# Attention scores of 64-row operands as paired products, in a one-core encoder layer

## The chip, the core and the metric

The kernel runs on one core of a Trainium2 chip. The metric is the time of one execution on the device, in microseconds (us); the profile is of one further execution, taken by the hardware profiler. TensorE appears in the profile as PE (products) and PEld (loads of the stationary operand), VectorE as DVE, ScalarE as ACT, GpSimd as POOL, SyncE as SP.

## What is computed

One encoder layer over 256 tokens of width 2048, in float32: adaLN modulation, a mixer with two attention groups of eight heads each, an output projection, a squared-ReLU feed-forward of width 8192, and a final norm. The change is in the scores of both groups:

```python
def diff_attention(q, k, v, lam):
    scale = DIFF_HEAD_DIM ** -0.5
    def block(qb):
        s = jnp.einsum('bqhcd,bkhcd->bhcqk', qb * scale, k).astype(jnp.float32)
        p = jax.nn.softmax(s, axis=-1)
        a = p[:, :, 0] - lam32 * p[:, :, 1]
        return jnp.einsum('bhqk,bkhe->bqhe', a.astype(v.dtype), v)

def mla_attention(q_nope, q_rope, k_nope, k_rope, v):
    scale = (MLA_NOPE_DIM + MLA_ROPE_DIM) ** -0.5
    def block(args):
        qn, qr = args
        s = (jnp.einsum('bqhd,bkhd->bhqk', qn, k_nope)
             + jnp.einsum('bqhr,bkr->bhqk', qr, k_rope)).astype(jnp.float32) * scale
        p = jax.nn.softmax(s, axis=-1)
        return jnp.einsum('bhqk,bkhe->bqhe', p.astype(v.dtype), v)
```

A differential head has two maps (c = 0, 1), each from queries and keys of 64 elements. A latent head adds a product over 128 elements (the plain part) and one over 64 rotary elements whose key is shared by all heads.

## The kernel before

All tensors lie with 128 partitions. Tokens come in two blocks of 128 (`t` = 0, 1). Weights stream from memory in pieces of 1 MB through a ring of buffers (`raw_tile`); for the large projections each piece is split on ScalarE and VectorE into a high and a low part (`split`, L124 and L125) and multiplied in three products (`block`, L299). The adaLN vectors are made beside that, from a stream of their own: part of it as products on TensorE with 32 columns in each of four column groups of the array (`ada_cols`, L319, and `ada_pe`, L382), part of it as multiply-adds on VectorE (`ada_acc`, L366) that GpSimd or TensorE then sums over partitions.

The stages follow each other: adaLN and input projection, latent attention's preparation (`latent_prep`), the attention itself, the output projection (`mixer_out`), the feed-forward. `run(...)` mixes generators by weights and so sets the order in which the instructions are written; a scheduler with tile dependencies then orders each engine's queue, and each engine works through its queue in that order.

`attention()` goes through heads 0 to 7 of both groups together. For each even head it first makes keys, values and queries of a latent pair (`latent_kv`, `latent_q`), then, for each head, the latent scores, the differential scores and, two heads later (`LAG` = 2), the transposes of the probabilities and the products with the values.

The scores are float32 products without the split, and each is two passes in the trace. The pieces that the change touches:

- Differential scores, L650 to L675. `diff_heads_T` transposes query and key of a head into one bank `pt` (`dT`), both maps above each other: rows 0 to 63 are map 0, rows 64 to 127 map 1. The query goes to `qT` (`dqT`, L657). The key goes into `kz` in two halves, each beside zeros that GpSimd wrote once: map 0 by ScalarE (L659), map 1 by VectorE (L660). `diff_scores` then makes one product of 128 rows and 512 columns per token block, with both maps beside each other in one bank `ds` (L667).
- Latent scores, L600 to L613. Per head and token block one product of 128 rows for the plain part (L605) and one of 128 rows for the rotary part (L606), into the same bank `ms`. The rotary query `qr` holds both heads of a pair above each other, and the key `krz` holds the shared key once for each head beside zeros.
- `softmax_rows`, L591 to L598: the negated row maximum on VectorE (L593), its product with the scale (L594), two exponentials on ScalarE with that as bias and the scale as factor (L596), a reciprocal of the sums (L598). For the differential maps follow the factor `nlam` (L671), a scaling on ScalarE (L672) and a multiply-add on VectorE (L673).

## Time and profile before

| | |
|---|---|
| median of 3 runs | 1188.09 us (1187.98 to 1190.48) |
| span of the profiled execution, first to last instruction | 1182.8 us |
| its own time | shown by the span alone; the runs' median is 5.3 us above it |
| instructions | 14208 |
| TensorE busy, products | 1140.9 us, 96% |
| TensorE busy, weight loads | 916.1 us, 77% |
| VectorE busy | 811.8 us, 69% |
| ScalarE busy | 552.0 us, 47% |
| GpSimd busy | 53.3 us, 5% |
| read from memory | 294.47 MB, 251 GB/s over the span |

Shares over the span mix stages with different limits, so the busy time is also read by stretches. A product that has been issued overlaps the one before it: the distance between two starts, not the duration of one, says how long TensorE is taken by it.

### The profile page before, as it was taken

What the parts mean: (1) busy time and instruction counts of PE and PEld (TensorE: products, weight loads), DVE (VectorE), ACT (ScalarE), POOL (GpSimd) and SP (SyncE); (2) the same over time, 40 slices, a digit from 0 to 9 for tenths busy, and PEclk for the clock granted to TensorE, in tenths of its full rate; (3) what the DMA queues carried; (4) which work ended last, traced back from release to release, by engine and by line L of the source; (5) the groups of instructions that cost most, each with busy time, mean ns of one, the idle gap of its engine ahead of it and who ended that gap; (6) DMA issues with size and microseconds to landing.
All of it is one profiled execution on the core that took longest, in us unless ns stands there. A gap on an engine that the chain in (4) does not pass through costs nothing.

```text
span 1182.8 us, 14208 instructions
## 1 busy us (share of the span) xinstructions
PE 1140.9 (96%) x5502; PEld 916.1 (77%) x5502; DVE 811.8 (69%) x1013; ACT 552.0 (47%) x812; POOL 53.3 (5%) x50
## 2 busy tenths in 40 slices
PE   5999999998999998999999999999999999999996
PEld 4666778865778887888888888888888888888875
DVE  3245559996899878875755666676686676555776
ACT  3432334547774445445544444344344344344343
POOL 1000000112101000000000000000020002000000
PEclk9999999999999998999999999999999999999998
DMA  9999973786888786996565646667767867556531
GB/s 348 392 390 369 356 305 130 254 313 223 292 313 299 281 315 236 330 343 219 185 220 178 209 155 205 236 232 266 276 222 275 281 237 251 184 181 203 182 104 72
DMA packets 94196, 297.50 MB, mean 252 GB/s; under 512 B 5712, under 2 KB 16167, under 8 KB 93488
## 3 DMA queue, kind: packets, MB, share of 16 engines
q1 hardware_dynamic: 94016, 296.56, 71.1%
q8 instruction: 43, 0.70, 0.2%
q14 instruction: 25, 0.20, 0.0%
q10 hardware_dynamic: 112, 0.03, 0.0%
HBM read 294.47 MB, written 2.10 MB: 251 GB/s over the span
## 4 chain that ended last, share of the span: by engine, by line
PE 60%; DVE 1%; issue 1%; ACT 0%; ACTq 0%; POOLq 0%; POOL 0%; DVEq 0%
PE f_p L299 51%; PE f1a_p L299 7%; PE fT L903 1%; PE h2T L856 0%; DVE x_res L921 0%; DVE acc L920 0%; DVE acc L918 0%; PE shift_f_pc L407 0%; PE scale_f_pc L407 0%; DVE acc L924 0%; ACT sq L927 0%; DVE h2t L829 0%; ACT acc L840 0%; ACT acc L948 0%; PE h2Ts L845 0%
## 5 line engine op out<-in xcount | busy, mean ns | idle before, releaser
L125 DVE TENSOR_TENSOR f_w_lo<-f_r,f_w_hi 128x1024 fp32r<-128x1024 f32 x224 | 278.1, 1250 | 197.4 <-ACT f_w_hi L124 197.0
L124 ACT CAST f_w_hi<-f_r 128x1024 fp32r<-128x1024 f32 x224 | 236.2, 1054 | 317.8 <-PE f_p L299 300.9
L299 PE MATMUL f_p<-f_w_hi,h 128*128 128x512 f32 x768 | 209.4, 391 | 0.0
L299 PEld LDWEIGHTS f_p<-f_w_hi,h 128*128 128x128 f32 x768 | 143.4, 188 | 29.3 <-ACT h L859 0.2
L299 PE MATMUL f_p<-f_w_hi,fh 128*128 128x512 f32 x512 | 158.6, 390 | 0.3 <-ACT fh L905 0.3
L299 PE MATMUL f_p<-f_w_lo,fh 128*128 128x512 f32 x512 | 158.8, 389 | 0.0
L299 PE MATMUL f_p<-f_w_hi,fl 128*128 128x512 f32 x512 | 158.8, 389 | 0.0
L299 PE MATMUL in_p<-in_w_hi,hT 128*128 128x512 f32 (+1 forms) x512 | 141.5, 389 | 2.8 <-ACT hT L354 2.7
L299 PE MATMUL f_p<-f_w_lo,h 128*128 128x512 f32 x384 | 119.0, 390 | 0.0
L299 PEld LDWEIGHTS in_p<-in_w_hi,hT 128*128 128x128 f32 x512 | 95.9, 191 | 26.9 <-ACT in_w_hi L124 4.3
L299 PEld LDWEIGHTS f_p<-f_w_hi,fh 128*128 128x128 f32 x512 | 96.0, 188 | 21.9 <-DVE acc L918 1.4
L299 PEld LDWEIGHTS f_p<-f_w_hi,fl 128*128 128x128 f32 x512 | 96.0, 188 | 20.0
L299 PEld LDWEIGHTS f_p<-f_w_lo,fh 128*128 128x128 f32 x512 | 96.1, 188 | 19.8
L125 DVE TENSOR_TENSOR in_w_lo<-in_r,in_w_hi 128x1024 fp32r<-128x1024 f32 (+1 forms) x64 | 73.2, 1169 | 44.5 <-ACT in_w_hi L124 44.2
L299 PEld LDWEIGHTS f_p<-f_w_lo,h 128*128 128x128 f32 x384 | 72.0, 188 | 14.8
L299 PE MATMUL in_p<-in_w_lo,hT 128*128 128x512 f32 (+1 forms) x256 | 79.5, 389 | 1.7 <-DVE in_w_lo L125 1.5
L124 ACT CAST in_w_hi<-in_r 128x1024 fp32r<-128x1024 f32 (+1 forms) x64 | 62.8, 1011 | 34.9 <-PE in_p L299 27.3
L299 PE MATMUL f1a_p<-f1a_w_hi,h 128*128 128x512 f32 x256 | 70.1, 394 | 0.0
L299 PEld LDWEIGHTS in_p<-in_w_lo,hT 128*128 128x128 f32 x256 | 48.1, 191 | 12.4 <-DVE in_w_lo L125 5.2
L299 PEld LDWEIGHTS f1a_p<-f1a_w_hi,h 128*128 128x128 f32 x256 | 48.4, 190 | 9.9
L124 ACT CAST f1a_w_hi<-f1a_r 128x1024 fp32r<-128x1024 f32 x32 | 33.6, 1054 | 42.3 <-PE f1a_p L299 34.9
L124 ACT CAST out_w_hi<-out_r 128x1024 fp32r<-128x1024 f32 x32 | 33.6, 1053 | 38.4 <-PE out_p L299 38.4
(323 smaller groups left out, 1380.0 us busy)
## 6 DMA issues: line engine op xcount, KB each, us to landing
f_r<-w_ff SPq DMA_DIRECT2D x112, 1024.0 KB, 5.5
in_r<-w_in SPq DMA_DIRECT2D x24, 1024.0 KB, 11.4
sc__r<-w_ada SPq DMA_DIRECT2D x16, 1024.0 KB, 10.4
sh__r<-w_ada SPq DMA_DIRECT2D x16, 1024.0 KB, 6.7
gate_m_r<-w_ada SPq DMA_DIRECT2D x16, 1024.0 KB, 5.9
scale_f_r<-w_ada SPq DMA_DIRECT2D x16, 1024.0 KB, 5.1
out_r<-w_out SPq DMA_DIRECT2D x16, 1024.0 KB, 8.2
shift_f_r<-w_ada SPq DMA_DIRECT2D x16, 1024.0 KB, 6.3
```

The costliest lines, as they stand in the source:

```text
L124: s.copy(hi, src)
L125: v.tensor_tensor(lo, src, hi.bitcast(F32), ALU.subtract)
L299: pe.matmul(ps[t][j][:, 0:nw], lhsT=lhs[(lk0 + kk) // 8][:, (lk0 + kk) % 8, t * P:(t + 1) * P], rhs=rhs[:, n0:n0 + nw], start=(kk == 0 and ...
L903: pe.transpose(pt[:, i * S + t * P:i * S + (t + 1) * P], rl[:, t, (kp + i) * P:(kp + i + 1) * P], ident)
```

## The change

- The zero-padded keys `kz` and `krz` go, with their clears on GpSimd.
- `diff_heads_T` puts query and key into one tile `qkT`, both by ScalarE, and multiplies the query by the scale on the way. `diff_scores` takes rows 0 to 63 for map 0 and rows 64 to 127 for map 1: four products of 64 rows and 256 columns per head, map by map into two banks, so that a bank holds one map for both token blocks where it held both maps of one block. The two maps are combined after both softmaxes.
- `latent_scores` does both heads of a pair at once, with a bank each: per token block the rotary products of 64 rows, one per head, then the two plain products of 128 rows. The rotary key `kr` is one copy of the key above another.
- The scales go into the operands: the differential one into the query, the latent one into the plain key (the copy in `latent_kv`) and into `kr` (`latent_prep`). `softmax_rows` loses its scaling of the maxima.

```diff
@@ -60,6 +60,7 @@
 FW = (42.0, 2.0, 2, 2)
 PRI_ATT = 0
 
+MLA_SCALE = float((NOPE + ROPE) ** -0.5)
 TWO_PI = 2.0 * np.pi
 INV_2PI = float(np.float32(1.0 / TWO_PI))
 RND = 12582912.0
@@ -483,7 +484,7 @@
     mla_g = act.tile([P, D], F32, tag="x1", name="mla_g")
     swap = mla_g[:, 0:P]
     qx = mla_g[:, 256:512]
-    krz = mla_g[:, 512:1024].rearrange("p (a q) -> p a q", a=2)
+    kr = mla_g[:, 512:768]
     qn_ring = [mla_g[:, 1024 + i * 512:1024 + (i + 1) * 512].rearrange("p (a q) -> p a q", a=2) for i in range(2)]
     for i in range(4):
         g.tensor_copy(swap[:, i * 32:(i + 1) * 32], ident[:, (i ^ 1) * 32:(i ^ 1) * 32 + 32])
@@ -496,7 +497,6 @@
         return t1, t2
 
     def latent_prep():
-        g.memset(krz, 0.0)
         kpd = []
         for t in range(T):
             for nm, o, n in (("q", 0, QL), ("kv", QL, KVL)):
@@ -530,8 +530,8 @@
                 pe.transpose(pt[:, o * S + t * P:o * S + (t + 1) * P],
                              kpd[t][:, 2 * o:2 * o + 2, :].rearrange("p a b -> p (a b)"), ident)
         t1, t2 = rope_T(pt, "kr")
-        v.tensor_tensor(krz[0:64, 0, :], t1[0:64, :], t2[0:64, :], ALU.add)
-        v.tensor_tensor(krz[64:128, 1, :], t1[64:128, :], t2[64:128, :], ALU.add)
+        v.tensor_tensor(t1, t1, t2, ALU.add)
+        s.mul(kr, t1, MLA_SCALE)
         yield 0.5
 
     def three(ps, pairs):
@@ -551,7 +551,7 @@
             three(pk[:, i * S:(i + 1) * S],
                   [((hi[:, k, i, 0:P], lo[:, k, i, 0:P]), (cq_hi[:, nq + k, :], cq_lo[:, nq + k, :]))
                    for k in range(nkv)])
-        s.copy(kn[hp % 2], pk.rearrange("p (h q) -> p h q", h=2))
+        s.mul(kn[hp % 2], pk.rearrange("p (h q) -> p h q", h=2), MLA_SCALE)
         yield 1.3
         pv = bank(f"pv{hp}")
         for t in range(T):
@@ -588,29 +588,35 @@
         v.tensor_tensor(qr, t1, t2, ALU.add)
         hold.append((qn, qr))
 
-    def softmax_rows(sc, scale, p, sums, name):
+    def softmax_rows(sc, p, sums, name):
         nm = small.tile([P, 2], F32, tag="nm", name=name + "_nm")
         v.tensor_reduce(nm, sc, AX.X, ALU.max, negate=True)
-        v.tensor_scalar(nm, nm, scale, None, op0=ALU.mult)
         for i in range(2):
-            s.activation(p[:, i, :], sc[:, i, :], AF.Exp, bias=nm[:, i:i + 1], scale=scale,
+            s.activation(p[:, i, :], sc[:, i, :], AF.Exp, bias=nm[:, i:i + 1], scale=1.0,
                          accum_out=sums[:, i:i + 1])
         v.reciprocal(sums, sums)
 
-    def latent_scores(h, qn, qr):
-        i = h % 2
-        kh = kn[h // 2 % 2][:, i, :]
-        sc = bank(f"ms{h}", "mm")
-        for t in range(T):
-            pe.matmul(sc[:, t * S:(t + 1) * S], lhsT=qn[:, i, t * P:(t + 1) * P], rhs=kh, start=True, stop=False)
-            pe.matmul(sc[:, t * S:(t + 1) * S], lhsT=qr[:, t * P:(t + 1) * P], rhs=krz[:, i, :],
-                      start=False, stop=True)
-        p = p_buf()
-        sums = small.tile([P, 2], F32, tag="sums", name=f"msum{h}")
-        softmax_rows(sc.rearrange("p (t k) -> p t k", t=2), float((NOPE + ROPE) ** -0.5), p, sums, f"m{h}")
-        for t in range(T):
-            s.mul(p[:, t, :], p[:, t, :], sums[:, t:t + 1])
-        return p
+    def latent_scores(hp, qn, qr):
+        scs = [bank(f"ms{2 * hp + i}", "mm") for i in range(2)]
+        for t in range(T):
+            for i in range(2):
+                hs = slice(64 * i, 64 * i + 64)
+                pe.matmul(scs[i][:, t * S:(t + 1) * S], lhsT=qr[hs, t * P:(t + 1) * P], rhs=kr[hs, :],
+                          start=True, stop=False)
+            for i in range(2):
+                pe.matmul(scs[i][:, t * S:(t + 1) * S], lhsT=qn[:, i, t * P:(t + 1) * P], rhs=kn[hp % 2][:, i, :],
+                          start=False, stop=True)
+        ps = []
+        for i in range(2):
+            h = 2 * hp + i
+            p = p_buf()
+            sums = small.tile([P, 2], F32, tag="sums", name=f"msum{h}")
+            softmax_rows(scs[i].rearrange("p (t k) -> p t k", t=2), p, sums, f"m{h}")
+            for t in range(T):
+                s.mul(p[:, t, :], p[:, t, :], sums[:, t:t + 1])
+            ps.append(p)
+            yield 1.8
+        lps.extend(ps)
 
     def latent_probs_T(h, p):
         tp = bank(f"mtp{h}")
@@ -653,33 +659,38 @@
             for t in range(T):
                 pe.transpose(pt[:, o * S + t * P:o * S + (t + 1) * P],
                              qk[t][:, o * 1024 + h * P:o * 1024 + (h + 1) * P], ident)
-        qT = at.tile([P, S], F32, tag="dqT", name=f"dqT{h}", bufs=2)
-        s.copy(qT, pt[:, 0:S])
-        z = kz[h % 2]
-        s.copy(z[0:64, 0, :], pt[0:64, S:2 * S])
-        v.tensor_copy(z[64:128, 1, :], pt[64:128, S:2 * S])
-        return qT, z
-
-    def diff_scores(h, qT, z):
-        ps = []
-        for t in range(T):
-            sc = bank(f"ds{h}{t}", "mm")
-            pe.matmul(sc, lhsT=qT[:, t * P:(t + 1) * P], rhs=z.rearrange("p a b -> p (a b)"), start=True, stop=True)
+        qkT = qkT_ring[h % 2]
+        s.mul(qkT[:, 0, :], pt[:, 0:S], float(DH ** -0.5))
+        s.copy(qkT[:, 1, :], pt[:, S:2 * S])
+        return qkT
+
+    def diff_scores(h, qkT):
+        scs = [bank(f"ds{h}{c_}", "mm") for c_ in range(2)]
+        for t in range(T):
+            for c_ in range(2):
+                hs = slice(64 * c_, 64 * c_ + 64)
+                pe.matmul(scs[c_][:, t * S:(t + 1) * S], lhsT=qkT[hs, 0, t * P:(t + 1) * P], rhs=qkT[hs, 1, :],
+                          start=True, stop=True)
+        ps, sm = [], []
+        for c_ in range(2):
             p = p_buf()
-            sums = small.tile([P, 2], F32, tag="sums", name=f"dsum{h}{t}")
-            softmax_rows(sc.rearrange("p (t k) -> p t k", t=2), float(DH ** -0.5), p, sums, f"d{h}{t}")
-            v.tensor_tensor(sums[:, 1:2], sums[:, 1:2], nlam, ALU.mult)
-            s.mul(p[:, 0, :], p[:, 0, :], sums[:, 0:1])
-            v.scalar_tensor_tensor(p[:, 0, :], p[:, 1, :], sums[:, 1:2], p[:, 0, :], op0=ALU.mult, op1=ALU.add)
+            sums = small.tile([P, 2], F32, tag="sums", name=f"dsum{h}{c_}")
+            softmax_rows(scs[c_].rearrange("p (t k) -> p t k", t=2), p, sums, f"d{h}{c_}")
             ps.append(p)
-        return ps
-
-    def diff_probs_T(h, ps):
+            sm.append(sums)
+        v.tensor_scalar(sm[1], sm[1], nlam, None, op0=ALU.mult)
+        for t in range(T):
+            s.mul(ps[0][:, t, :], ps[0][:, t, :], sm[0][:, t:t + 1])
+            v.scalar_tensor_tensor(ps[0][:, t, :], ps[1][:, t, :], sm[1][:, t:t + 1], ps[0][:, t, :],
+                                   op0=ALU.mult, op1=ALU.add)
+        return ps[0]
+
+    def diff_probs_T(h, p):
         tp = bank(f"dtp{h}")
         pT = pT_buf()
         for t in range(T):
             for kt in range(T):
-                pe.transpose(tp[:, kt * S + t * P:kt * S + (t + 1) * P], ps[t][:, 0, kt * P:(kt + 1) * P], ident)
+                pe.transpose(tp[:, kt * S + t * P:kt * S + (t + 1) * P], p[:, t, kt * P:(kt + 1) * P], ident)
         s.copy(pT, tp.rearrange("p (k q) -> p k q", k=2))
         return pT
 
@@ -769,7 +780,7 @@
     if LAG > 1:
         p_ring += [lat[t][:, 0:512].rearrange("p (a q) -> p a q", a=2) for t in range(T)]
         p_ring.append(at.tile([P, 2, S], F32, tag="px", name="px"))
-    kz = [asc[1][:, 1024 + i * 512:1024 + (i + 1) * 512].rearrange("p (a q) -> p a q", a=2) for i in range(2)]
+    qkT_ring = [asc[1][:, 1024 + i * 512:1024 + (i + 1) * 512].rearrange("p (a q) -> p a q", a=2) for i in range(2)]
     cnt = {"p": 0, "pT": 0}
 
     def p_buf():
@@ -780,8 +791,8 @@
         cnt["pT"] += 1
         return at.tile([P, 2, S], F32, tag="pT", name=f"pT{cnt['pT']}", bufs=2)
 
-    for z in kz:
-        g.memset(z, 0.0)
+    lps = []
+
     def attention():
         live = []
         for i in range(H + LAG):
@@ -789,13 +800,13 @@
                 if i % 2 == 0 and i > 0:
                     yield from latent_kv(i // 2)
                     yield from latent_q(i // 2, hold)
-                lp = latent_scores(i, *hold[i // 2])
-                yield 1.8
+                if i % 2 == 0:
+                    yield from latent_scores(i // 2, *hold[i // 2])
             if i >= LAG:
                 lT = latent_probs_T(i - LAG, live[0][0])
                 yield 0.5
             if i < H:
-                live.append((lp, diff_scores(i, *diff_heads_T(i))))
+                live.append((lps[i], diff_scores(i, diff_heads_T(i))))
                 yield 2.0
             if i >= LAG:
                 dT = diff_probs_T(i - LAG, live.pop(0)[1])
```

Two places of the instruction order bear on the prediction. The first is TensorE at heads 2 and 3, before (`ms2` and `ms3` are the latent score banks of these heads, `ds20` and `ds21` the differential ones of head 2, first by token block, then by map; `mo` and `do` are products with the values):

```order
L606 MATMUL ms2_2258<-mla_g_1502,qr1_2252 128x256
L605 MATMUL ms2_2258<-mla_f_1501,mla_g_1502 128x256
L606 MATMUL ms2_2258<-mla_g_1502,qr1_2252 128x256
L667 MATMUL ds20_2294<-asc1_2052,dqT2_2290 128x512
L667 MATMUL ds21_2306<-asc1_2052,dqT2_2290 128x512
L627 MATMUL mo0_2325<-pT1_2283,mla_f_1501 128x256 x2
L690 MATMUL do0_2330<-dv0_93,pT2_2319 128x128
L690 MATMUL do0_2330<-dv1_94,pT2_2319 128x128
L690 MATMUL do0_2330<-dv0_93,pT2_2319 128x128
L690 MATMUL do0_2330<-dv1_94,pT2_2319 128x128
L605 MATMUL ms3_2337<-mla_f_1501,mla_g_1502 128x256
```

and now, from the second token block's latent scores on:

```order
L604 MATMUL ms2_2247<-mla_g_1502,qr1_2241 128x256
L604 MATMUL ms3_2248<-mla_g_1502,qr1_2241 128x256
L607 MATMUL ms2_2247<-mla_f_1501,mla_g_1502 128x256
L607 MATMUL ms3_2248<-mla_f_1501,mla_g_1502 128x256
L672 MATMUL ds20_2293<-asc1_2051 128x256
L672 MATMUL ds21_2294<-asc1_2051 128x256
L672 MATMUL ds20_2293<-asc1_2051 128x256
L672 MATMUL ds21_2294<-asc1_2051 128x256
L633 MATMUL mo0_2323<-pT1_2284,mla_f_1501 128x256 x2
L701 MATMUL do0_2328<-dv0_93,pT2_2317 128x128
```

The latent scores of head 3 stood behind head 2's differential scores and the value products; now they alternate with head 2's, two rotary products of 64 rows and two plain ones of 128, and the differential scores of head 2 follow as four products that alternate between two banks.

The second is VectorE while the first two heads are scored, before (`kv_lo` and `q_0_lo` are low parts of the next latent pair's weights, `m_nm` and `d_nm` the row maxima):

```order
L125 TENSOR_TENSOR kv_lo<-kv_r_2163,kv_hi 128x1024
L594 TENSOR_SCALAR d_nm<-d_nm 128x2
L598 RECIPROCAL dsum_2085<-dsum_2085 128x2
L593 TENSOR_REDUCE m_nm<-ms_2107 128x2
L671 TENSOR_TENSOR dsum_2085<-dsum_2085,nlam 128x1
L593 TENSOR_REDUCE d_nm<-ds_2130 128x2
L673 SCALAR_TENSOR_TENSOR asc_2051<-asc_2051,dsum_2085 128x256
L594 TENSOR_SCALAR m_nm<-m_nm 128x2
L594 TENSOR_SCALAR d_nm<-d_nm 128x2
L593 TENSOR_REDUCE d_nm<-ds_2142 128x2
L598 RECIPROCAL dsum_2097<-dsum_2097 128x2
L125 TENSOR_TENSOR q_0_lo<-q_r_2197,q_0_hi 128x768
```

and now:

```order
L593 TENSOR_REDUCE m_nm<-ms_2053 128x2
L367 SCALAR_TENSOR_TENSOR gate_m_1671<-gate_m_r_2071,cs,gate_m_1671 128x1024
L593 TENSOR_REDUCE m_nm<-ms_2054 128x2
L367 SCALAR_TENSOR_TENSOR gate_m_1671<-gate_m_r_2071,cs,gate_m_1671 128x1024
L597 RECIPROCAL msum_2063<-msum_2063 128x2
L126 TENSOR_TENSOR kv_lo<-kv_r_2152,kv_hi 128x1024
L597 RECIPROCAL msum_2075<-msum_2075 128x2
L126 TENSOR_TENSOR q_0_lo<-q_r_2186,q_0_hi 128x768
L126 TENSOR_TENSOR q_1_lo<-q_r_2186,q_1_hi 128x768
L593 TENSOR_REDUCE d_nm<-ds_2090 128x2
```

The scalings of the maxima between the rows are gone, and both low parts of the query weight stand ahead of the first maximum of the differential scores.

## Rows read from the trace of the kernel before

**Rows 1.** The page, part 1 (engine, busy us, share, instructions) and part 4 (chain).

```profile
PE 1140.9 (96%) x5502; PEld 916.1 (77%) x5502; DVE 811.8 (69%) x1013; ACT 552.0 (47%) x812; POOL 53.3 (5%) x50
...
PE 60%; DVE 1%; issue 1%; ACT 0%; ACTq 0%; POOLq 0%; POOL 0%; DVEq 0%
PE f_p L299 51%; PE f1a_p L299 7%; PE fT L903 1%; PE h2T L856 0%; DVE x_res L921 0%; DVE acc L920 0%; DVE acc L918 0%; PE shift_f_pc L407 0%; PE scale_f_pc L407 0%; DVE acc L924 0%; ACT sq L927 0%; DVE h2t L829 0%; ACT acc L840 0%; ACT acc L948 0%; PE h2Ts L845 0%
```

**Rows 2.** Stretches of the span: length; busy us by engine; granted clock, DMA share, GB/s.

```profile
50.00:100.00 50.00, 48.29 (x269) 31.85 (x267) 21.01 (x29) 17.41 (x25) 0.00 (x0) 1.00 1.05 386
250.00:300.00 50.00, 44.85 (x257) 30.33 (x256) 39.02 (x88) 37.62 (x107) 11.72 (x6) 1.00 0.68 235
300.00:350.00 50.00, 48.12 (x287) 36.01 (x286) 47.13 (x91) 37.95 (x114) 3.59 (x1) 1.00 0.91 327
350.00:400.00 50.00, 49.46 (x241) 41.18 (x240) 43.86 (x52) 24.08 (x30) 5.70 (x3) 1.00 0.84 304
600.00:700.00 100.00, 100.00 (x450) 82.59 (x449) 54.53 (x54) 45.36 (x52) 0.00 (x0) 1.00 0.58 190
```

**Rows 3.** TensorE's waits at 250 to 350 us: total us, times, longest.

```profile
PE pq L542 <- DVE q_lo L125: 3.4, 1, 3.4
PE dtp L682 <- ACT qk L693: 1.5, 1, 1.5
```

**Rows 4.** Timeline of TensorE, 252 to 260 us: start, duration, instruction, count.

```profile
252.10 0.59 PE L605 MATMUL ms<-mla_f,mla_g 128*128 128x256 f32 x2
252.53 0.59 PE L606 MATMUL ms<-mla_g,qr 128*128 128x256 f32 x2
253.06 1.07 PE L382 MATMUL gate_m_pg<-gate_m_r,cpad 128*32 128x512 f32 x8
...
257.83 1.98 PE L667 MATMUL ds<-asc,dqT 128*128 128x512 f32 x4
```

**Rows 5.** Timeline of TensorE, 330 to 350 us.

```profile
332.63 1.88 PE L667 MATMUL ds<-asc,dqT 128*128 128x512 f32 x4
334.35 1.05 PE L690 MATMUL do<-dv,pT 128*128 128x128 f32 x8
```

**Rows 6.** Score products, by form, 250 to 350 us: busy us, mean ns.

```profile
L667 PE MATMUL ds<-asc,dqT 128*128 128x512 f32 x32 | 15.5, 606 | 0.1
...
L606 PE MATMUL ms<-mla_g,qr 128*128 128x256 f32 x32 | 9.8, 389 | 0.0
```

**Rows 7.** Timeline of TensorE, 88 to 94 us (input projection, adaLN, input projection).

```profile
88.31 1.07 PE L299 MATMUL in_p<-in_w_hi,hT 128*128 128x512 f32 x4
...
89.67 0.61 PE L299 MATMUL in_p<-in_w_hi,hT 128*128 128x512 f32 x2
90.22 1.92 PE L319 MATMUL sh__pg<-sh__r,cpad 128*32 128x512 f32 x16
92.07 1.21 PE L299 MATMUL in_p<-in_w_hi,hT 128*128 128x512 f32 x4
```

**Rows 8.** VectorE's groups by form, 245 to 350 us: busy us, mean ns, idle.

```profile
L594 DVE TENSOR_SCALAR d_nm<-d_nm 128x2 f32<-128x2 f32 x16 | 5.0, 319 | 0.0
...
L660 DVE COPY asc<-dT 64x256 f32<-64x256 f32 x8 | 3.4, 428 | 0.6 <-ACT asc L659 0.3
...
L671 DVE TENSOR_TENSOR dsum<-dsum,nlam 128x1 f32<-128x1 f32 x16 | 2.4, 151 | 0.1
```

**Rows 9.** ScalarE's group of query copies, same view and stretch.

```profile
L657 ACT COPY dqT<-dT 128x256 f32<-128x256 f32 x8 | 3.1, 392 | 0.4 <-PE dT L654 0.4
```

**Rows 10.** Timeline of VectorE, 261 to 270 us.

```profile
262.18 2.21 DVE L594 TENSOR_SCALAR d_nm<-d_nm 128x2 f32<-128x2 f32 x1
...
268.64 0.93 DVE L125 TENSOR_TENSOR q_lo<-q_r,q_hi 128x768 fp32r<-128x768 f32 x1
...
269.87 0.15 DVE L594 TENSOR_SCALAR d_nm<-d_nm 128x2 f32<-128x2 f32 x1
```

**Rows 11.** Timeline of GpSimd, 250 to 300 us.

```profile
262.06 6.55 POOL L393 PARTITION_ALL_REDUCE gate_m<-gate_m  x2 [9.62 <-DVE d_nm L593]
```

## Prediction

> **What bounds the kernel now.** I read the page first. TensorE is busy for 96% of the span and VectorE for 69%; the chain that ended last runs through 60% of the span and is TensorE throughout [rows 1]. So time that TensorE gains in a stage where it is the engine that runs on can reach the end, if nothing after it was waiting for something else. The busy time by stretches says where that holds [rows 2]: the attention stage lies at about 250 to 350 us, with TensorE busy 44.85 and 48.12 of each 50 us, VectorE 39.02 and 47.13; behind it TensorE goes on at 49.46 of 50, and in the feed-forward (600 to 700 us) at 100 of 100, all at a granted clock of 1.00 (2.4 GHz). The DMA queues moved 386 GB/s at 50 to 100 us and 327 and 304 GB/s at 300 to 400 us, so the weights can come a few microseconds sooner. The waits of TensorE inside the stage name what else can end last [rows 3]: 3.4 us once for a half of a query weight on VectorE, 1.5 us once before a transpose of probabilities. A saving in TensorE's work is therefore worth nearly its face value; a wait that the change creates costs the same.
>
> **TensorE: the paired products.** A float32 product stands in the trace as two passes. The passes of 256 columns follow each other 0.215 us apart (two start at 252.10, the next two at 252.53 [rows 4]), those of 512 columns 0.43 us (four from 332.63 to 334.35 [rows 5]). There are 32 passes of 512 columns of the differential scores (`ds`, L667) and 32 of 256 columns of the rotary half of the latent scores (`ms`, L606) [rows 6]: 13.8 + 6.9 = 20.6 us. The change makes each a product over 64 rows, 256 columns, in the upper or lower half of the array, and gives the two of a pair a bank each. If both halves stream at once, the 20.6 us become 10.3. No row shows two row halves at once. The nearest row is the adaLN product that uses four groups of 32 columns: eight passes of 512 columns take 1.07 us there, against 1.98 us for four of `ds` [rows 4], so four groups did stream side by side, both passes included. I take full overlap: 10.3 us gained. The other end is no overlap: nothing.
>
> **TensorE: the changes of tiling.** The same adaLN product shows what it costs to go from the whole array to a part and back. Dense passes follow each other 0.23 us apart (four take 1.07, two 0.61); the last dense one began at 89.67 + 0.23 = 89.90, the first tiled one at 90.22 [rows 7]: 0.32, so 0.1 too late. On the way back four dense passes take 1.21 us instead of 1.07 [rows 7], because the first weights are loaded in the open, and they begin about 0.1 us after the 16 tiled passes (4 x 0.43 us) are through. A first weight load of 128 columns in the open shows again in `ds` after the adaLN product, where four passes take 1.98 instead of 1.88 us [rows 4, 5]. So a change of tiling costs about 0.1 of idling and 0.1 of open weight load, 0.2 us each way. The Trainium skill, TensorEngine Tiling (Array Packing), section Tiling Modes, says that changing the mode, not merely the tile, drains TensorE; the trace agrees, with the 0.1 us above. By that rule the sum is the one below; without it the gain would be the whole 10.3 us.
>
> In the new order there are 15 stretches of 64-row products: two for each of the four latent pairs (rotary, plain, rotary, plain) and seven for the eight differential heads, the first two heads standing together. That is 30 changes, one of which takes the place of one that was there: 29 x 0.2 = 5.8 us. Bounds for one change: 0 (products of unlike lines in the same tiling follow without a gap [rows 5]) and 0.4 (twice the measured). It is instructive that the latent half pays nothing: per token block it saves 0.43 us and buys two changes for 0.4. The gain is the differential half. TensorE's work: -10.3 + 5.8 = -4.5 us.
>
> **VectorE and ScalarE.** Gone from VectorE are 24 scalings of the row maxima (16 of them of `ds`), 0.15 us each where nothing disturbs them [rows 10], 8 copies of half a key, 0.43 us each, and 8 of 16 small products of 0.15 us [rows 8]: 3.6 + 3.4 + 1.2 = 8.2 us of an engine that is busy 86 of 100 us here. A scaling stood between each row maximum and its exponentials, and a key copy on VectorE ahead of each `ds`; both sat in VectorE's queue among adaLN's long passes. ScalarE now copies the whole key (128 rows by 256) where it copied half of it, at the 0.39 us that the query copy takes [rows 9], and scales `kr` once: some 0.5 us in all, on an engine with 12 of 50 us free [rows 2]. The removed GpSimd clears waited for nothing that anyone needed. These edits cost nothing while that cover lasts. On the debit side, a head's two maps must now both be through their softmax before either token block is combined, and both heads of a latent pair are scored before the first transposes; what would then be late is a transpose of probabilities two heads on, 1.5 us in one place now.
>
> Of TensorE's waits, 3.4 us are one event: GpSimd's two all-reduces run from 262.06 for 6.55 us [rows 11], a VectorE operation on 2 columns takes 2.21 us meanwhile, and the query half that TensorE needs is begun only at 268.64 [rows 10]. In the new VectorE order both query halves stand ahead of the first `ds` maxima, so they may be done before the all-reduces start, or be caught by them. Of 3.4 + 1.5 = 4.9 us I take 1.5 as gone: between all of it and nothing, nearer to nothing, because the new order opens waits of its own at this place (the key and query copies of the first two differential heads now stand behind the first latent pair's softmax on ScalarE).
>
> **The sum.** -4.5 - 1.5 = -6.0 us. The profiled execution has a span of 1182.8 us, 5.3 below the runs' median of 1188.09; what lies around the span is taken as unchanged. Span 1176.8, time **1182.1 us**.
>
> **Rivals.**
> - *The waits go too.* All 4.9 us vanish, since VectorE loses a tenth of its work: -4.5 - 4.9, 1178.7. For it: the 3.4 us are one collision. Against: the all-reduces still run, with new neighbours.
> - *Half overlap.* If passes start strictly in program order, the second pass of the first product holds up the second product: a pair takes 3 rounds of 0.215 us instead of 2, four products 5 instead of 4. Saved: 8 x 0.65 + 8 x 0.215 = 6.9 instead of 10.3; less 5.8 and with the 1.5: 1185.5. Against it speak the eight passes in 1.07 us [rows 4], which strict order with 0.43 us per round would not allow. The Trainium skill, TensorE: Matmul & The Clock Gate, Part 3, states that matmuls are strict FIFO in start and end; how a float32 product's two passes are queued it does not say.
> - *The gain becomes a wait.* TensorE arrives sooner, but the softmax chain of VectorE and ScalarE ends when it did: about 1188. Against: those engines lose work too.
> - *Slower: the pairs do not pack.* The products over 64 rows run one after the other, so the change does not do what it says. Place: the `ms` rotary pairs and all `ds`. TensorE keeps its 20.6 us and pays 5.8 us: 1193.9. It decides from the point where less than 5.8 of the 10.3 us is saved. Against: the column groups overlap, and each half has its own bank; for: no row shows it for rows.
>
> **How the numbers follow.** Forecast 0.53, waits too 0.14, half overlap 0.11, gain becomes a wait 0.10, slower 0.12. Faster by over 0.2% (2.4 us, about what a measurement of this kernel tells from no change) means below 1185.7: nearly all of the forecast, the first rival, and half of the second: 0.70. Within: 0.17. Slower: 0.13. Range: down to the free changes of tiling (-10.3 - 1.5: 1176.3) and up past the costly ones (0.4 each: -10.3 + 11.6 - 1.5, 1187.9) and the lost gain to 1189.5; the unpacked case is left out.
>
> **What would show it.** Right: the two products of a pair start within some 0.02 us; the four `ds` of a head take about 1.1 us with their change in, instead of 1.72; the rotary pair 0.43; plain products after it start 0.1 us late with an open load; no scaling between maximum and exponential; from 400 us on the same work, shifted by 6 us. Wrong: `ds` passes 0.215 us apart one by one, or new waits of TensorE over 3 us before `ds`, `pk` or `dtp`.

## The result, and the profile after

The changed kernel takes **1193.39 us** (median; 1192.95 to 1194.88), the kernel before, run beside it, 1188.03: a ratio of 1.0055, 95% interval 1.004 to 1.0071. It is slower by half a per cent, where 1182.1 was forecast. The profiled execution has a span of 1191.1 us against 1182.8.

Those two spans are 8.3 us apart, the medians 5.4. The table ahead of the prediction takes 5.3 us as lying between span and time; in every run whose span stands beside its time the difference is 1.7 to 1.9 us. So the profiled execution of the kernel before was a quick one of its kind: beside the experiments the same kernel ran 80 times, with a median span of 1186.0 us and a mean granted clock of 0.989 over the span (0.986 to 0.992), where the profiled execution has 1182.8 and 0.991. The four runs of the changed kernel all have 0.982.

TensorE's line on the page, and the granted clock in the span's 40 slices (page, parts 1 and 2, of the changed kernel):

```profile
PE 1144.5 (96%) x5534; PEld 918.7 (77%) x5534; DVE 807.3 (68%) x972; ACT 552.5 (46%) x813; POOL 50.2 (4%) x47
...
PEclk9999999988989998999999999999999999999999
```

TensorE is busy 3.6 us *longer* than in [rows 1], with less to do. The clock's tenths show four slices at 8, three of them in the attention stage (in the kernel before one at the mixer's end, and the last slice of all). The same stretches as [rows 2] (length; busy us of PE, PEld, DVE, ACT, POOL; granted clock; DMA share; GB/s), and then every stretch at a granted clock of 0.50 in which TensorE works:

```profile
250.00:300.00 50.00, 44.55 (x255) 30.68 (x254) 33.55 (x67) 37.47 (x106) 10.68 (x4) 0.86 0.61 212
300.00:350.00 50.00, 42.69 (x273) 29.90 (x272) 43.13 (x62) 32.79 (x95) 3.45 (x1) 0.96 0.84 309
...
25.09:31.92 6.83, 5.81 (x17) 5.54 (x18) 2.82 (x4) 1.96 (x4) 0.00 (x0) 0.50 1.03 393
260.58:267.41 6.83, 5.41 (x22) 4.02 (x23) 6.61 (x7) 3.41 (x8) 5.49 (x3) 0.50 0.94 333
287.89:294.71 6.82, 6.06 (x22) 4.41 (x23) 1.86 (x5) 3.27 (x10) 3.23 (x1) 0.50 0.41 156
345.91:352.74 6.83, 6.35 (x23) 4.70 (x24) 5.27 (x8) 5.12 (x14) 0.00 (x0) 0.50 0.80 279
451.73:458.56 6.83, 4.32 (x15) 3.01 (x16) 5.14 (x11) 5.42 (x15) 1.31 (x2) 0.50 0.47 154
550.72:554.13 3.41, 3.41 (x10) 2.62 (x11) 2.84 (x7) 1.83 (x5) 0.00 (x0) 0.50 0.52 154
```

The kernel before has two of them, at the start and behind the mixer:

```profile
25.60:32.43 6.83, 6.03 (x17) 5.77 (x18) 2.59 (x4) 2.18 (x4) 0.00 (x0) 0.50 1.03 392
445.50:452.33 6.83, 5.10 (x16) 3.69 (x17) 5.15 (x10) 5.33 (x12) 0.81 (x1) 0.50 0.46 156
```

If half of the busy time at 1.2 GHz counts as lost against 2.4 GHz, a span splits into three parts that can be compared: the loss (half the busy time of such stretches), the work (busy time of the page less the loss), the idle time (span less busy time). Before: loss (6.03 + 5.10) / 2 = 5.6, work 1135.3, idle 41.9. After: loss 31.36 / 2 = 15.7, work 1128.8, idle 46.6. So **work -6.5, loss +10.1, idle +4.7: +8.3 us**, the difference of the spans. The products were saved; the clock and new waits took more than that. How exact the split is, and that it charges the clock too much, is read from the experiments' table.

The idle time is in TensorE's waits at 240 to 365 us (total us, times, longest), to be held against [rows 3]:

```profile
PE mo L633 <- ACT pT L627: 5.0, 1, 5.0
PE pk L542 <- DVE kv_lo L126: 3.6, 1, 3.6
PE pq L542 <- ACT qk L704: 1.8, 1, 1.8
PE dT L660 <- ACT qk L704: 1.7, 1, 1.7
```

The clock falls inside the 3.6, the 1.7 and the 5.0 (at 260.58, 287.89 and 345.91 us). TensorE's timeline shows what the three cost and what the pairs bring (start, duration, instruction, count, idle before it):

```profile
262.00 0.58 PE L542 MATMUL pk<-cq,kv_lo 128*128 128x256 f32 x1 [3.61 <-DVE kv_lo L126]
...
262.94 3.79 PE L672 MATMUL ds<-asc 64*128 64x256 f32 x16
...
278.07 0.70 PE L604 MATMUL ms<-mla_g,qr 64*128 64x256 f32 x4
278.70 1.13 PE L607 MATMUL ms<-mla_f,mla_g 128*128 128x256 f32 x4
279.76 0.70 PE L604 MATMUL ms<-mla_g,qr 64*128 64x256 f32 x4
280.39 1.13 PE L607 MATMUL ms<-mla_f,mla_g 128*128 128x256 f32 x4
281.45 1.13 PE L672 MATMUL ds<-asc 64*128 64x256 f32 x8
282.52 0.70 PE L633 MATMUL mo<-pT,mla_f 128*128 128x256 f32 x2
...
288.65 1.11 PE L660 MATMUL dT<-ident,qk 128*128 128x128 f32 x4 [1.71 <-ACT qk L704]
...
346.39 1.22 PE L633 MATMUL mo<-pT,mla_f 128*128 128x256 f32 x2 [5.01 <-ACT pT L627]
347.54 2.08 PE L672 MATMUL ds<-asc 64*128 64x256 f32 x8
```

The `ds` of a head (eight passes of 64 rows) take 1.07 us to the next start at 281.45; in [rows 5] they took 1.72. Behind the 5.0 us wait the same eight last 2.08 us, 1.13 at 281.45, and at 262.94 sixteen last 3.79: where the clock has fallen it takes more than the pairs save.

What stands ahead of the 3.6 us wait is VectorE's low part of the key weight beside GpSimd's all-reduces (timelines of the changed kernel, and the same operation before):

```profile
258.62 6.49 POOL L394 PARTITION_ALL_REDUCE gate_m<-gate_m  x2 [45.16 <-DVE gate_m L367]
258.73 3.22 DVE L126 TENSOR_TENSOR kv_lo<-kv_r,kv_hi 128x1024 fp32r<-128x1024 f32 x1
```

```profile
261.05 1.22 DVE L125 TENSOR_TENSOR kv_lo<-kv_r,kv_hi 128x1024 fp32r<-128x1024 f32 x1
```

The all-reduces now start 3.4 us sooner [rows 11], and the operation that they meet takes 3.22 us where it took 1.22.

What stands ahead of the 5.0 us wait is ScalarE's queue (its timeline):

```profile
339.73 0.48 ACT L595 ACTIVATE asc<-ms,m_nm 128x256 f32<-128x256 f32 x1 [1.90 <-DVE m_nm L593]
...
341.54 1.70 ACT L616 ACTIVATE asc<-asc,msum 128x256 f32<-128x256 f32 x4
343.13 0.47 ACT L595 ACTIVATE asc<-ds,d_nm 128x256 f32<-128x256 f32 x1
...
344.93 0.92 ACT L683 ACTIVATE asc<-asc,dsum 128x256 f32<-128x256 f32 x2
345.73 0.60 ACT L627 COPY pT<-mtp 128x512 f32<-128x512 f32 x1
```

Both latent heads of the pair (four exponentials, four scalings) and both maps of head 6 run without a pause for 6 us before `pT` is copied, for which TensorE has been waiting since 341.4, when its transposes were through.

### The profile page after: what moved, and what is told of

Read it like the earlier page. It is cut to its first block, busy times and chain, and to the rows that moved or that the text cites. A ratio compares the mean times of both kernels' runs of the same rounds, so it can differ in the third digit from the quotient of the medians.

```text
span 1191.1 us, 14212 instructions
## 1 busy us (share of the span) xinstructions
PE 1144.5 (96%) x5534; PEld 918.7 (77%) x5534; DVE 807.3 (68%) x972; ACT 552.5 (46%) x813; POOL 50.2 (4%) x47
## 4 chain that ended last, share of the span: by engine, by line
PE 60%; DVE 1%; issue 1%; ACT 0%; ACTq 0%; POOLq 0%; POOL 0%; DVEq 0%
PE f_p L300 51%; PE f1a_p L300 7%; PE fT L914 1%; PE h2T L867 0%; DVE x_res L932 0%; DVE acc L931 0%; DVE acc L929 0%; PE shift_f_pc L408 0%; PE scale_f_pc L408 0%; DVE acc L935 0%; ACT sq L938 0%; DVE h2t L840 0%; ACT acc L851 0%; ACT acc L959 0%; PE h2Ts L856 0%
## 5 line engine op out<-in xcount | busy, mean ns | idle before, releaser
L126 DVE TENSOR_TENSOR in_w_lo<-in_r,in_w_hi 128x1024 fp32r<-128x1024 f32 (+1 forms) x64 | 73.2, 1169 | 44.4 <-ACT in_w_hi L125 44.1
```

The costliest lines, as they stand in the source:

```text
L126: v.tensor_tensor(lo, src, hi.bitcast(F32), ALU.subtract)
```

## Experiments

The first theory: scoring both heads of a latent pair at once puts both softmaxes on ScalarE and VectorE ahead of work that TensorE waits for; it waits, and its clock falls. Four kernels took the change apart. Ratios are to the kernel before, run beside them.

**e1_diff_only.** The kernel before with `diff_heads_T`, `diff_scores` and `diff_probs_T` of the change, the differential scale in the query among them.

```diff
-            sc = bank(f"ds{h}{t}", "mm")
+        scs = [bank(f"ds{h}{c_}", "mm") for c_ in range(2)]
...
+                pe.matmul(scs[c_][:, t * S:(t + 1) * S], lhsT=qkT[hs, 0, t * P:(t + 1) * P], rhs=qkT[hs, 1, :],
```

> The kernel before with the differential half of the change alone: 64-row pairs in two banks, whole key copied, scale in the query, both maps through their softmax before they are combined; the latent half (zero-padded rotary key, one head after the other) as before. Theory (the loss comes from both heads of a latent pair going through their softmax one right after the other, which stands ahead of work that TensorE waits for, and the granted clock falls after the long waits): none of TensorE's waits of 3.6 to 5 us, no stretch of half clock between 32 and 445 us, and the packing's gain shows: 32 passes by 0.215 us less 16 changes of tiling by 0.2 = -3.6, about 1183 to 1185.5. Rival (the late combining of the two maps, or two banks for each head, makes the waits): the long waits and the half clock are there, 1191 to 1194.

Measured 1188.8 us, ratio 1.0015 (1.0003 to 1.0028): neither. Its work is 3.4 us less than before's, near the 3.6 expected; but there is a wait of 3.2 us for a copy of the head output on ScalarE (`dtp` for `qk`), half clock behind it at 337 us and again at 375 and 545 (loss +4.2, idle +2.3). The differential half makes waits too; the joint latent softmax is not their only source.

**e2_latent_only.** The changed kernel's `latent_scores`, with the differential half of the kernel before (the cut is against the kernel before).

```diff
-                lp = latent_scores(i, *hold[i // 2])
+                if i % 2 == 0:
+                    yield from latent_scores(i // 2, *hold[i // 2])
```

> The changed kernel's latent half (paired rotary products, both heads of a pair scored together, scales in the keys) with the differential half of the kernel before. Theory: TensorE's gain is about nothing (8 pairs save 0.43 us each and pay two changes of tiling each), the waits for pT, kv_lo, qk and the half clock behind them stay: 1191 to 1195. Rival (the differential half makes the waits): 1187 to 1189.

Measured 1194.16 us, ratio 1.0058 (1.0037 to 1.0079): the time as the theory had it, work -0.5, loss +3.3, idle +4.3. But the waits are others: 4.0 us of `dtp` for `qk`, 1.6 for `kv_lo`, 0.8 for `pT`. This half alone costs as much as the whole change.

**e3_split_softmax.** The changed kernel, the odd head's latent softmax in its own step.

```diff
-                    yield from latent_scores(i // 2, *hold[i // 2])
+                    pair_it = latent_scores(i // 2, *hold[i // 2])
+                yield next(pair_it)
```

> The changed kernel, with one edit: the odd head's latent softmax is issued in that head's own step, as before the change; the scores of the pair are still made together and in pairs. Theory: the ScalarE queue ahead of pT, qk and kv_lo is shorter by one softmax at each pair, the waits of 3.6 and 5 us fall to under 2, the clock stays at 1.00 in the attention stage, and TensorE's gain of 4.5 us shows: 1182 to 1186. Rival (changes of tiling or their cost are the loss): nothing moves, 1192 to 1195.

Measured 1186.73 us, ratio 0.9995 (0.9982 to 1.0007). Taking the joint softmax apart gives back the 6 us that the change lost: that is shown for this edit. Against the changed kernel loss is 7.5 us less and idle time 2.4. That the joint softmax is the cause by itself is not shown: e4 below has none and is as late as the change, e12 keeps it and is less late. Nor did the gain over the kernel before come, or waits under 2 us: one of 3.9 us (`dtp` for `qk`) came up, with half clock from inside it on; work -2.8, loss +2.6, idle +2.3.

**e4_scales_only.** The kernel before, no pairs, scales in query and keys.

```diff
-        v.tensor_scalar(nm, nm, scale, None, op0=ALU.mult)
...
-        s.copy(qT, pt[:, 0:S])
+        s.mul(qT, pt[:, 0:S], float(DH ** -0.5))
```

> The kernel before with only the scales put into the query (differential) and into the keys (latent): no scaling of the row maxima on VectorE; zero-padded keys, the order of the scores and TensorE's work as before. Both theories: VectorE has 24 operations of 0.15 us less, no wait of TensorE grows, the time is 1186 to 1189. A rival that puts the loss on the scales (ScalarE busier, kr and kn later) would see 1190 or more.

Measured 1193.31 us, ratio 1.0052 (1.0033 to 1.0071): a miss for both theories. It is the time of the rival that puts the loss on the scales, but not with its signs: ScalarE is busy 552.6 us, 552.0 before, and TensorE waits nowhere for a scaled key or query. TensorE's waits at 240 to 365 us sum to 7.5 us, 7.1 before, and idle time is 42.4 us, 41.9 before; but three new stretches of half clock stand in the stage (and one at 551 us):

```profile
257.45:260.86 3.41, 3.41 (x12) 1.23 (x5) 2.00 (x3) 2.46 (x9) 0.00 (x0) 0.51 0.81 240
271.10:274.50 3.40, 3.40 (x10) 1.51 (x10) 2.79 (x7) 3.40 (x11) 0.00 (x0) 0.51 0.46 131
346.20:349.60 3.40, 2.73 (x7) 2.27 (x8) 1.98 (x4) 3.17 (x8) 0.00 (x0) 0.51 0.52 164
```

Its loss is 6.1 us more than before's, and that is most of the slowdown. Taking VectorE's 24 scalings out bought nothing. The queues came out in another order, and the clock falls at waits no longer than 2.1 us; that the order is the reason is argued, not shown.

**e12_pairs_no_scales.** The complement of e4: the changed kernel with VectorE's scaling of the maxima back and the exponentials' scale with it.

> The changed kernel without the folding of the scales: the row maxima are scaled on VectorE as before the change, the exponentials take the scale, query and keys are copied unscaled. The pairs, the order of the scores and the late combining stay. If the scales are the loss (e4_scales_only was 6 us slower with them alone): 1186 to 1189. If the pairs and their softmax are: 1192 to 1196. If either edit by itself only shuffles which waits the clock falls behind, the two losses of 6 us do not add up to the change's 6, and the time lies anywhere in 1186 to 1196 with its half-clock stretches accounting for it.

Measured 1190.25 us, ratio 1.0024 (1.0014 to 1.0034), the third case of its expectation: the losses of the parts do not add up. Work -1.9, loss +4.7, idle +2.5.

So the second theory: TensorE's work falls as forecast; every re-ordered queue has other waits, and what decides is how long they are and whether the clock falls at them. Three runs (e6, e9, e7) tried to move single waits, two (e8, e10) the changes of tiling.

**e6_probs_first.** `latent_probs_T` written ahead of `latent_scores`.

> The changed kernel with one edit of order: the latent probabilities of two heads back are transposed and copied before the scores and the softmax of the next pair are issued, so that pT's copy no longer stands behind that pair's softmax on ScalarE. Theory (the joint softmax ahead of pT makes the 5.0 us wait of mo): that wait goes, with the fall of the clock behind it (3.2): 1185 to 1188. If the wait only moves to the next bank or copy that ScalarE is late with: 1190 or more.

Measured 1194.46 us, ratio 1.0049 (1.003 to 1.0068). The waits are those of the change to 0.4 us: the scheduler gave VectorE and ScalarE the same order, so the edit moved nothing. The run serves as a repeat of the changed kernel: its split (table below) differs by 0.4 us at most.

**e9_pT_prio.** The copy of the latent `pT` at a higher scheduling priority (`with tc.high_priority(offset=30)`).

> The changed kernel with a higher scheduling priority for the copy of the latent pT alone (priority raised by 30), which puts that copy ahead of the next pair's exponentials on ScalarE at the last pair; at the middle pairs it moves by a few places. Theory (the pair's softmax ahead of pT makes the 5.0 us wait, and the clock's fall at 346 us follows from that wait): the wait and that stretch of half clock go, 3 to 8 us less than the change: 1185 to 1190. Rival (another copy on ScalarE is late instead, dT's or the head output's): 1192 or more.

Measured 1192.82 us, ratio 1.0045 (1.0032 to 1.0058): the rival. `mo` no longer waits, `ds` behind it waits 4.1 us for the key copy on ScalarE (`asc` of `dT`), and the clock falls at 345 us as before. ScalarE's 6 us burst is late for whichever copy stands behind it.

**e7_split_dov.** e3, one of the two head output copies on VectorE; **e8_split_dov_group** and **e10_split_group**: e7 and e3 with the scores of a pair in the order plain, rotary, rotary, plain.

```diff
-            s.mul(qk[t][:, h * P:(h + 1) * P], po[:, t * P:(t + 1) * P], 2.0 ** -32)
+        v.tensor_scalar(qk[1][:, h * P:(h + 1) * P], po[:, P:2 * P], 2.0 ** -32, None, op0=ALU.mult)
...
+        plain(0, True)
+        rotary(0, False)
+        rotary(1, True)
+        plain(1, False)
```

> The kernel of e3_split_softmax, with one of the two copies of each differential head's output out of its bank (head output by 2^-32) moved from ScalarE to VectorE, which the change has relieved. Its waits of TensorE in the stage were 5.4 us for ScalarE's copies of that output; theory (ScalarE's bursts are what is late after the change): those waits fall under 2 and the clock falls less: 1180 to 1185. Rival (VectorE is no better placed): 1186 or more.

> The kernel of e7_split_dov, with the latent scores of a pair in the order plain, rotary, rotary, plain: one stretch of 64-row products for each pair in place of two, so 8 changes of tiling less. If a change costs the 0.2 us of the sum, 1.6 us less than e7_split_dov; if the changes cost nothing, the same as e7_split_dov.

> The kernel of e3_split_softmax with the latent scores of a pair in the order plain, rotary, rotary, plain: 8 changes of tiling less, all else by the scheduler's choice. Sum: 1.6 us less than e3_split_softmax, 1185; if the schedule around it turns worse, 1190 or more. It is the version that would beat both kernels.

Measured 1197.27 us (1.008; 1.0064 to 1.0095), 1194.39 (1.005; 1.0033 to 1.0067) and 1190.19 (1.002; 1.0011 to 1.0029). VectorE is no better placed: waits of 4.1, 2.9 and 2.5 us came up, and 6.1 us behind the mixer. Eight changes of tiling less took 2.4 us of work from e7 and 2.1 from e3 (1131.8 to 1129.4, 1132.5 to 1130.4), where 1.6 were expected (the split is not exact enough to tell these apart); but e10 is slower than e3, by the rival of its expectation: its loss is 4.2 us larger, with a wait of 6.1 us behind the mixer, and its queues came out in another order.

Is the fall caused by what TensorE leaves idle, or does it only go along with it? The next runs give TensorE useless products (the identity by a tile at hand, into a part of a bank that is written over afterwards or not read) inside a wait.

**e5_fill** and **e11_fill_pk.**

```diff
+    def filler(dst, n):
+        for _ in range(n):
+            pe.matmul(dst, lhsT=ident, rhs=kr, start=True, stop=True)
...
+        if hp == 1:
+            filler(pk[:, 0:S], 7)
```

> The changed kernel with useless products of TensorE (identity by kr, 256 columns, 0.43 us each, into a part of the next bank that is written over or not read) ahead of the three places where its trace waits before the clock falls: 7 before pk of the second pair (wait 3.6), 3 before dT of head 3 (wait 1.7), 9 before mo of head 5 (wait 5.0). 8.2 us more work, all of it inside waits. Theory (half of the loss and more is the granted clock that falls after those waits): the half-clock stretches at 260, 288 and 346 us go, the loss in them (2.7 + 3.0 + 3.2 = 8.9 us) comes back, less what the products overshoot the waits by (up to 1): 1184 to 1188. Rival (the waits themselves cost the time, the clock is a side effect that costs little): 1193 or more.

> The changed kernel with the 7 useless products (3.0 us) ahead of pk of the second pair alone, where e5_fill showed its 3.6 us wait filled. Theory (the granted clock falls for what TensorE leaves idle there, and costs the stretch that follows about 2.7 us): the 16 passes of ds behind it take 2.1 instead of 3.8 us, no half clock at 260 to 267 us, and 1 to 3 us less than the change: 1190 to 1192.5. Rival (the clock falls for another reason): half clock there as before, the same time or 1 more.

e5 measured 1202.14 us (1.0117; 1.0099 to 1.0135): a miss. Two of its three fillers stood in banks that were themselves what TensorE waited for, so they ran behind the wait and cost their own time. e11 has one filler only, and the queues' order of the changed kernel but for a few instructions; 1195.77 us (1.0068; 1.0055 to 1.0082). TensorE's timeline of e11:

```profile
256.52 3.29 PE L547 MATMUL pk<-mla_g,ident 128*128 128x256 f32 x14
...
261.62 0.38 PE L542 MATMUL pk<-cq,kv_lo 128*128 128x256 f32 x1 [0.60 <-DVE kv_lo L126]
261.85 0.39 PE L542 MATMUL pk<-cq,kv_hi 128*128 128x256 f32 x2
262.17 2.13 PE L678 MATMUL ds<-asc 64*128 64x256 f32 x16
...
272.59 0.39 PE L542 MATMUL pr<-cq 128*128 128x256 f32 x1 [1.95 <-ACT mla_f L560]
...
319.26 2.08 PE L639 MATMUL mo<-pT,mla_f 128*128 128x256 f32 x4 [2.92 <-DVE om L642]
```

The mechanism is right, the time is not: with the wait filled, sixteen `ds` passes take 2.13 us, not 3.79. But TensorE, 2.4 us ahead, then waits 1.95 for ScalarE and later 2.92 for VectorE, and the clock falls at both (273.6 and 318.0 us). In this stage the three engines pace each other: what TensorE gains at one place it waits for at the next.

**e13_after_fill_dtp** fills the 5.0 us wait of the changed kernel, **e14_split_fill_dT** the 3.9 us wait of e3, in banks that are free there; **e15_split_fill** and **e16_before_fill_h2** also the waits behind the mixer, on e14 and on the kernel before. The cut shows e14's and e15's fillers.

```diff
+        if h == 5:
+            filler(pt[:, 0:S], 8, kr)
...
             pt = bank(f"h2Ts{t}")
+            filler(pt[:, 0:P], 7 if t == 0 else 7, ident)
```

> The changed kernel with 9 useless products of TensorE (3.9 us) into the bank of the transposed differential probabilities of head 5, ahead of those transposes: inside the 5.0 us wait before mo (341 to 346 us), in a bank that is free there. Theory (what TensorE leaves idle makes the clock fall, and the fall costs more than the wait): no half clock at 346 to 353 us, its 3.2 us back: 1189 to 1191.5. Rival (the fall comes whatever TensorE does there, or another fall takes its place): 1192.5 or more.

> The kernel of e3_split_softmax with 8 such products (3.4 us) into the bank of head 5's query and key transposes, ahead of them: inside the 3.9 us wait before dtp at 310 to 314 us, every engine's order otherwise that of e3_split_softmax. Theory: no half clock at 314 to 320 us, its loss of 3.0 us back, less what the products overshoot: 1183 to 1185.5. Rival (a fall elsewhere takes its place, or none of it matters): 1186 or more.

> The kernel of e14_split_fill_dT, and 7 products of 128 columns (some 1.5 us) ahead of each of the two groups of transposes of h2 behind the mixer, where TensorE waits 1.9 us twice and the clock then falls (loss 3.5 us at 443 us). Theory: both stretches of half clock go; 3 us less than e14_split_fill_dT: 1180 to 1183, below both kernels. Rival: the same as e14_split_fill_dT or slower.

> The kernel before with the same products ahead of the transposes of h2 alone (its order of work is otherwise the same). It has one stretch of half clock there, which costs 2.5 us. Theory: that comes back less any overshoot, 1184.5 to 1186.5. Rival: 1187 or more.

e13: 1194.33 us, ratio 1.0052 (1.0035 to 1.0069). TensorE's timeline has the fall gone, and `ds` at 1.07 us again:

```profile
341.09 4.05 PE L547 MATMUL dtp<-mla_g,ident 128*128 128x256 f32 x18
344.98 0.60 PE L699 MATMUL dtp<-ident,px 128*128 128x128 f32 x4
346.69 1.13 PE L637 MATMUL mo<-pT,mla_f 128*128 128x256 f32 x4 [1.11 <-ACT pT L631]
347.75 1.14 PE L676 MATMUL ds<-asc 64*128 64x256 f32 x8
```

Loss 11.0 instead of 15.7; but the time did not follow. Of a lead of 1.7 us at `do` of head 6 most went in a new wait of 1.4 us for VectorE (`oT` for `mf`), and the other two falls of the stage stay. For the time this run is a miss.

e14: 1186.52 us, ratio 0.9983 (0.997 to 0.9995), every engine's order that of e3 but for the fillers. TensorE's timeline of e3, then of e14:

```profile
314.07 1.12 PE L691 MATMUL dtp<-ident,asc 128*128 128x128 f32 x4 [3.89 <-ACT qk L702]
...
317.46 2.08 PE L670 MATMUL ds<-asc 64*128 64x256 f32 x8
...
320.80 0.48 PE L542 MATMUL pk<-cq,kv_hi 128*128 128x256 f32 x2
```

```profile
309.60 3.62 PE L547 MATMUL dT<-mla_g,ident 128*128 128x256 f32 x16
...
314.09 0.65 PE L697 MATMUL dtp<-ident,asc 128*128 128x128 f32 x4 [0.43 <-ACT qk L708]
...
316.53 1.13 PE L676 MATMUL ds<-asc 64*128 64x256 f32 x8
...
318.51 0.48 PE L542 MATMUL pk<-cq,kv_hi 128*128 128x256 f32 x2
```

Up to the transposes behind the wait the two run alike (314.07 and 314.09); without the fall `pk` of the next pair starts 2.3 us sooner, where the split charges 3.0 for that stretch. The time is in the rival's range all the same (1186 or more): the clock now falls at 541 us, where e3 kept it, and behind the mixer TensorE waits 3.1 us for what it waited 1.9.

e15: **1183.53 us, ratio 0.9961 (0.9947 to 0.9976)**, half a microsecond above its range; e16: 1185.7, ratio 0.9981 (0.9968 to 0.9993), in its range, with every engine's order that of the kernel before but for the fillers. In their profiled executions neither has any half clock from 50 us to the end of the work. For e15 the view by stretches, whole and behind the mixer:

```profile
50.00:1175.00 1125.00, 1107.00 (x5358) 891.49 (x5356) 789.98 (x945) 531.77 (x783) 48.55 (x33) 1.00 0.71 247
443.30:453.54 10.24, 8.79 (x51) 6.83 (x51) 8.89 (x15) 7.76 (x19) 1.13 (x1) 1.00 0.53 189
```

and for e16, where the kernel before's row above had a clock of 0.50:

```profile
445.50:452.33 6.83, 5.36 (x35) 3.95 (x34) 5.48 (x11) 5.59 (x14) 1.13 (x1) 1.00 0.46 154
```

The products compute nothing, and none of these four kernels is slower for them (e14's interval overlaps e3's, e13's that of the change). e15 is faster than both kernels of this case. That the clock falls for what TensorE leaves idle is thus shown at four places (e11, e13, e14, e16), in e14 and e16 with nothing else re-ordered. Not every fall is of that kind (last section). The granted clock over the span says the same of all runs: 0.990 to 0.992 in e14 against 0.987 to 0.990 in e3, 0.990 to 0.994 in e16 against 0.986 to 0.992 in the kernel before. In the kernel before, time goes with the clock where the program is the same: of its 80 runs the 27 at 0.990 or more have a median of 1185.9 us, the 19 at 0.987 or less one of 1189.9. What is not shown is that the clock alone made the change late: filling one of its waits (e11, e13) made the changed kernel no faster.

The three parts of the spans, in us, the fillers' own time within the work:

| kernel | span | work | loss | idle |
|---|---|---|---|---|
| before | 1182.8 | 1135.3 | 5.6 | 41.9 |
| after | 1191.1 | 1128.8 | 15.7 | 46.6 |
| e1 | 1185.9 | 1131.9 | 9.8 | 44.2 |
| e2 | 1189.9 | 1134.8 | 8.9 | 46.2 |
| e3 | 1184.9 | 1132.5 | 8.2 | 44.2 |
| e4 | 1191.6 | 1137.5 | 11.7 | 42.4 |
| e6 | 1191.3 | 1128.8 | 15.5 | 47.0 |
| e11 | 1195.5 | 1132.5 | 13.4 | 49.6 |
| e12 | 1188.1 | 1133.4 | 10.3 | 44.4 |
| e13 | 1190.4 | 1134.4 | 11.0 | 45.0 |
| e14 | 1183.4 | 1135.6 | 5.4 | 42.4 |
| e15 | 1180.2 | 1139.3 | 1.7 | 39.2 |
| e16 | 1183.6 | 1139.5 | 3.0 | 41.1 |

Work should be the same where the products are. It is not: e4 stands 2.2 us above the kernel before, e3 3.7 above the changed kernel, and it is least in the change and its repeat e6, where the loss is greatest. So the split charges the clock too much: part of what runs at half clock covers a wait that TensorE would otherwise have had (at e14 2.3 us for 3.0, and `mo` there waits 0.7 us for `pT` where it waits 0.3 in e3). The two kernels that keep their clock behind 50 us have 1132.7 (e15) and 1136.4 us (e16) of work without the fillers. With these as the work after and before, an estimate, the +8.3 us of the spans are work -3.7, loss +7.3, idle +4.7. And since the kernel before usually runs at a lower clock than in its profile, still less of the 5.4 us between the medians is the clock's: clock and waits may then weigh about the same, and which is the larger is not shown.

## Why the prediction was wrong

- **The paired products: right.** Full overlap was taken; the two products of a pair stream together (`ds` of a head 1.07 us with its changes of tiling, against 1.72).
- **The changes of tiling: right.** A rotary stretch takes 0.63 us to the next start (278.07 to 278.70) for 0.43 us of products: 0.2, and the plain one behind it 1.06 for 0.86: 0.2. The sum was -4.5 us of TensorE work. The split gives -6.5 for the changed kernel, -2.8 for e3 with the same products, and -3.7 between e15 and e16 less their fillers (16 passes of 0.216 and 28 of 0.112 us in e15, the 28 in e16), which the split's error touches least.
- **VectorE's relief: right in direction, wrong in worth.** Over the span VectorE is busy 4.5 us less (811.8 [rows 1] to 807.3), in e3 7.1 less; 8.2 were counted. In the changed kernel its passes beside the all-reduces take longer (3.22 for 1.22 us above). e4 and e12 show that leaving the scalings out bought nothing by itself.
- **"A saving in TensorE's work is therefore worth nearly its face value": this step failed.** It was read from TensorE's 45 to 48 busy us in 50 [rows 2]. But a busy share says nothing of who is second: e11 shows that TensorE, 2.4 us early, waits for ScalarE and VectorE at the next two places.
- **The waits: this term failed in sign.** 1.5 us were credited as gone; idle time grew by 4.7. The place was named ("what would then be late is a transpose of probabilities two heads on"), but the cover was called sufficient ("these edits cost nothing while that cover lasts"). It did not last: ScalarE's 6 us burst stands ahead of `pT`. The "12 of 50 us free" were an average; the pair's softmax comes at once. The 3.4 us at the all-reduces became 3.6: they start sooner and now meet `kv_lo`, one of the two outcomes that the prediction left open. Its own sign of being wrong, a new wait over 3 us before `pk`, came true there.
- **The clock: this term was missing.** [rows 2] show 1.00 throughout, and the sum took that as given, from a profiled execution that kept its clock better than most of its kernel. It cost +10.1 us by the split and some 7 by the estimate above, either of them more than the 4.5 us that were to be gained. The Trainium skill, TensorE: Matmul & The Clock Gate, section HAM oscillation — how this bites in real kernels, describes work that restarts at half rate after a wait for data; the prediction cited that page for queueing alone. The trace agrees, with waits of 3.6 and 5.0 us for VectorE and ScalarE in place of a DMA's.
- **The rivals.** "The pairs do not pack" gives 1193.9, nearly the measured time, by luck: the pairs do pack. "The gain becomes a wait" had the right first half; what lay beyond 1188 was new waits and the clock.
- **The 5.3 us around the span: misread, without harm.** What lies around it is 1.8 us; the rest is that the profiled execution was a quick one. The forecast was counted from the runs' median, so its time does not change.

What stays open: why the same wait is followed by a fall in one kernel and not in another. The kernel before waits 3.4 us [rows 3] and its clock stays at 1.00; the changed kernel waits 1.7 us at 287 and it falls; e11 has the same 1.7 us and there it does not. Why the new orders of the queues came out as they did was not tried, and neither was a kernel with the change's products in the order of the kernel before.

## What to carry to other kernels

Where TensorE is busy 95% of a stage, look at what it waits for next before crediting a saving, and look at the granted clock: here each fall cost 1.4 to 3.5 us by the split, so a few of them undo a gain of 4 us. After an edit that makes a scheduler order the queues anew, split the span into work at full clock, half-clock loss and idle time; without that, a right saving and a wrong one look alike. Take such a split as rough, and ask first whether the profiled execution is like the others of its kernel. Where a wait cannot be removed, products that compute nothing, in a bank that is free during it, may keep the clock up: they were worth 0.2% on the kernel before, and a third of a per cent with the split softmax (e3 to e15, ratios 0.9995 and 0.9961).

## What was not expected of the hardware

The clock also fell to 1.2 GHz at 550 us in the changed kernel, behind 16 one-column products (`shift_f_pc`) and eight transposes, with no wait over 0.2 us; the kernel before does the same work there at 2.4 GHz. It falls there in eleven of the eighteen profiles of this case, so the cost of such a place is not the same in two kernels that differ elsewhere alone.
